# A two-block network on one core: rope and query norm worked in other places, head pairs, and steps moved

## The chip, the cores and the metric

The program runs on one core of one Trainium2 chip. The metric is the device time of one execution in microseconds (us). The engines are TensorE (PE, with its weight loads PEld), VectorE (DVE), ScalarE (ACT), GpSimd (POOL) and SyncE (SP), which here only issues DMAs. Each engine works through its own queue in the order in which the program was written; SP's DMAs are one queue too.

## The reference

The input is 256 rows of 1024 numbers. Block one is attention plus PEER, block two has two layers. What matters here:

```python
# block one, attention half
q = (rms_norm(cq, cq_norm) @ w_uq).reshape(b, s, 8, 96)
kv = (rms_norm(ckv, ckv_norm) @ w_ukv).reshape(b, s, 8, 128)
k = concat([k_nope, broadcast(k_pe)], -1)        # 64 + 32, k_pe shared by the heads
q, k = rms_norm(q, q_norm), rms_norm(k, k_norm)  # over the 96 of a head
q, k = (concat([z[..., :64], rope(z[..., 64:], positions)]) for z in (q, k))
mla = chunk_causal_softmax_attention(q, k, v)    # beside it a stick-breaking attention, 8 heads of 64
x = x + concat([rms_norm(sb), rms_norm(mla)]) @ w_o
x = x + peer_ffn(rms_norm(x), ...)
# block two, layer 0: differential attention of 6 heads of 128, and a Fourier part of 256 columns
o = rmsnorm(o, subln_g) * (1 - lambda_init)      # each head by itself
x = x + gate * (concat([o, fourier_groups(f)]) @ w_out)
x = x + gate * swiglu(modulate(rmsnorm(x)))      # 2816 wide
# layer 1: convolution mixer and the same FFN; shift, scale and gate are silu(c) @ ada_w + ada_b
```

## The kernel before, in words

Activations lie transposed: 128 features on the partitions, 8 tiles of 256 rows (`xT`). Each product of full precision is three fast ones: every weight tile of 128x1024 is loaded by SP (`_load`, a ring of four), rounded on ScalarE (`_hi`) and its remainder taken on VectorE (`_lo`); `next_w` (L650) hands out the next tile of the order in `plan` (L532) and emits the casts of the tiles that follow, `self.los` remainders ahead. An output tile is then 24 matmuls. The code is written for a manual schedule: program order is queue order on each engine.

`first_mixer` (L835). `Pre` norms `xT` (L365): the first `raws` output tiles are computed from rows that are not yet normalized, while the norm is worked out, and are multiplied by the row factor `r` afterwards; later tiles read the normalized rows `hh`, `hl`. Six tiles come first: three of the query latent `cq`, two of the key and value latent `ckv`, and the shared rope key `kpe`, the sixth. Then four tiles of the stick-breaking values (48 matmuls of 512 columns). `rope_tables` (L771) is a generator of eight steps that works out sine and cosine of the angles; a step of it is emitted at each `next(rope)`, and `pre.side` emits one inside the first tile.

The attention itself is ordered by `weave` (L253): a main stream (weights in the order of `MAINS`) and tasks (the norms of queries and keys of two heads, `qk_norm` L1077, softmax heads `mla` L1102, stick-breaking heads) that a planner places into one order by a model of the engines' times. `qk_norm` squares 112x512 on ScalarE, sums with a product over ones on TensorE, takes logarithm and exponential over 112x512 and scales on VectorE; for queries it adds rope on VectorE and GpSimd.

`diff` (L1429) is the differential mixer, with the same planner: keys and second values, Fourier, then output tiles of `ev_out` are the main stream; units of heads are tasks. A pair of heads is normed by `pair`. The last two output tiles come after the planned part, in `acc_last` (L718). `ada` (L1375) is a generator of 48 steps, each one load of 512 KB and one VectorE pass, for the modulation vectors of layer 1; its steps are called out at places in `diff` and `ffn` (L1679), each `next(steps)`. `ffn` runs 22 rounds of two up tiles and one down tile and ends with `acc_last`; the first one also makes the 81 diagonal weights of the convolution and sets up the norm (`Pre`) of the mixer after it.

## Time and profile before

| what | value |
| --- | --- |
| time, median of 3 runs | 1707.84 us (1704.6 to 1708.96) |
| the profiled execution, its own time | 1705.88 us |
| its span | 1704.1 us |
| TensorE busy | 1642.9 us, 96% |
| VectorE busy | 1335.9 us, 78% |
| ScalarE busy | 1012.8 us, 59% |
| GpSimd busy | 321.9 us, 19% |

The span is from the first instruction to the last; the run's own time has 1.8 us around it. Busy time of TensorE is modelled at the ends of matmuls, so a matmul's row can be longer than its distance to the next one. Times in rows count from the span's start. Tiles are named by the program's names; `a` is the arena that most tiles share, so neighbours tell which one it is.

### The profile page before, as it was taken

How to read it: one execution, taken by the hardware profiler on the slowest of the kernel's cores; microseconds unless marked ns; L12 is line 12 of the kernel's file. 1: busy time of each engine (PE TensorE's matmuls, PEld its weight loads, DVE VectorE, ACT ScalarE, POOL GpSimd, SP SyncE). 2: the span in 40 equal slices, each digit the busy share in tenths (PEclk: the TensorE clock that was granted, in tenths of full speed). 3: DMA queues.
4: the chain of work that ended last, by engine and by line, in shares of the span. 5: the costliest groups of instructions: out<-in, count | busy, mean ns of one | idle time of the engine just before them, and what ended most of it. 6: DMA issues, size and time to landing. Idle time of an engine off the chain costs nothing.

```text
span 1704.1 us, 33577 instructions
## 1 busy us (share of the span) xinstructions
PE 1642.9 (96%) x12984; PEld 1577.0 (93%) x12984; DVE 1335.9 (78%) x2379; ACT 1012.8 (59%) x1932; POOL 321.9 (19%) x201
## 2 busy tenths in 40 slices
PE   6999999999999999999999999998999989899998
PEld 6878999999999999999999998787999989789997
DVE  6688899987788876778788879977878799875555
ACT  5875554567777765444555564565556677564444
POOL 1021589920000000000000015311000047310000
PEclk9999999999999999999999999999999999999999
DMA  5433455554444457767887753143898733245553
GB/s 179 129 112 100 143 171 177 183 169 162 161 162 162 162 169 244 244 235 247 301 299 278 259 195 134 56 149 134 296 307 313 260 112 100 65 158 186 186 186 124
DMA packets 88111, 315.66 MB, mean 185 GB/s; under 512 B 10000, under 2 KB 11024, under 8 KB 87696
## 3 DMA queue, kind: packets, MB, share of 16 engines
q1 hardware_dynamic: 87952, 313.51, 54.6%
q8 instruction: 104, 1.70, 0.4%
q14 instruction: 55, 0.45, 0.1%
HBM read 312.03 MB, written 1.05 MB: 184 GB/s over the span
## 4 chain that ended last, share of the span: by engine, by line
PE 73%; DVE 11%; ACT 6%; DMA 4%; POOL 3%; issue 2%; SPq 0%; DVEq 0%; ACTq 0%; POOLq 0%
PE mm L178 42%; PE at L178 30%; DVE a L208 9%; ACT a L208 3%; POOL a L208 3%; DMA a<-in_peer_v_dram 2%; ACT wh L208 2%; DMA a<-in_w_dram 1%; DMA a<-in_peer_u_dram 1%; DVE adaw L208 0%; DVE xT L208 0%; ACT L208 0%; DVE gb L208 0%; PE at L183 0%; DMA a<-in_w_in_dram 0%
## 5 line engine op out<-in xcount | busy, mean ns | idle before, releaser
L178 PE MATMUL mm<-a,wh 128*128 128x256 f32 (+3 forms) x4752 | 658.7, 288 | 19.6 <-DVE a L208 7.4
L208 ACT ACTIVATE wh<-a 128x1024 fp32r<-128x1024 f32 (+3 forms) x491 | 515.1, 1053 | 267.0 <-DMA a<-in_w_dram 116.9
L208 DVE TENSOR_TENSOR a<-a,wh 128x1024 fp32r<-128x1024 f32 (+2 forms) x436 | 539.0, 1243 | 124.2 <-ACT wh L208 123.2
L178 PEld LDWEIGHTS mm<-a,wh 128*128 128x128 f32 (+1 forms) x4752 | 602.7, 189 | 35.3 <-DVE a L208 10.1
L178 PE MATMUL mm<-a,a 128*128 128x256 f32 (+5 forms) x2616 | 413.1, 296 | 10.8 <-DVE a L208 7.7
L178 PEld LDWEIGHTS mm<-a,a 128*128 128x128 f32 (+1 forms) x2616 | 357.6, 191 | 22.2 <-DVE a L208 5.7
L178 PE MATMUL at<-a,wh 128*128 128x256 f32 x2152 | 283.0, 282 | 8.8 <-DVE a L208 4.9
L178 PEld LDWEIGHTS at<-a,wh 128*128 128x128 f32 x2152 | 268.2, 189 | 11.1 <-DVE a L208 5.7
L208 POOL TENSOR_TENSOR a<-a 128x256 f32<-128x256 f32 (+4 forms) x44 | 71.6, 1628 | 852.0 <-ACT a L208 826.6
L178 PE MATMUL at<-a,a 128*128 128x256 f32 (+6 forms) x1288 | 209.1, 296 | 3.3 <-DVE sz L208 1.9
L178 PEld LDWEIGHTS at<-a,a 128*128 128x128 f32 (+2 forms) x1288 | 170.6, 189 | 17.4 <-issue 12.8
L208 ACT ACTIVATE a<-a 128x256 fp32r<-128x256 f32 (+8 forms) x225 | 103.1, 469 | 115.4 <-DVE a L208 86.0
L208 POOL TENSOR_TENSOR a<-a,a 128x256 f32<-128x256 f32 (+4 forms) x65 | 77.8, 1201 | 476.6 <-ACT a L208 422.5
L208 POOL TENSOR_TENSOR a<-a,wh 128x1024 fp32r<-128x1024 f32 x54 | 148.6, 2773 | 15.4 <-ACT wh L208 15.2
L208 DVE TENSOR_TENSOR a<-a,a 128x256 fp32r<-128x256 f32 (+6 forms) x188 | 108.3, 577 | 28.7 <-ACT a L208 23.8
L208 ACT ACTIVATE a<-mm 128x256 f32<-128x256 f32 (+30 forms) x174 | 60.6, 352 | 96.5 <-PE mm L178 96.2
L178 PE MATMUL at<-fgh,wh 128*128 128x256 f32 x352 | 87.3, 284 | 2.2 <-ACT wh L208 2.2
L178 PE MATMUL at<-fgl,wh 128*128 128x256 f32 x352 | 87.1, 284 | 0.0
L208 ACT ACTIVATE oh<-oh,rest 128x128 f16<-128x128 f16 x256 | 81.1, 399 | 0.0
L208 DVE TENSOR_TENSOR a<-a,at 128x204 f32<-128x204 f32 (+54 forms) x115 | 36.6, 355 | 48.9 <-PE at L178 42.6
L208 DVE TENSOR_TENSOR fs<-fs,mm 128x256 f32<-128x256 f32 x38 | 16.0, 421 | 74.5 <-PE mm L178 69.0
L178 PEld LDWEIGHTS at<-fgh,wh 128*128 128x128 f32 x352 | 67.1, 191 | 2.7 <-ACT wh L208 2.7
(157 smaller groups left out, 1559.4 us busy)
## 6 DMA issues: line engine op xcount, KB each, us to landing
a<-in_w_dram SPq DMA_DIRECT2D x132, 512.0 KB, 3.5
a<-in_peer_u_dram SPq DMA_DIRECT2D x128, 512.0 KB, 3.3
a<-in_peer_v_dram SPq DMA_DIRECT2D x128, 512.0 KB, 4.2
adaw<-in_ada_dram SPq DMA_DIRECT2D x48, 512.0 KB, 4.4
a<-in_ada_dram SPq DMA_DIRECT2D x48, 512.0 KB, 5.0
a<-in_pw_dram SPq DMA_DIRECT2D x24, 512.0 KB, 3.3
a<-in_w_pq_dram SPq DMA_DIRECT2D x16, 512.0 KB, 3.2
a<-in_ev_qkf_dram SPq DMA_DIRECT2D x14, 512.0 KB, 3.3
```

Source lines behind the costliest of these rows:

```text
L178: return self.engine.matmul(out, w, x, **kw)
L208: return f(*args, **kw)
```

## The change

It makes six edits. The rope key is computed as a sixth raw tile and scaled by `r` on VectorE; the angle steps move out of the first tiles into the four value tiles. The keys of two heads come from one product of 128 weight columns. The query norm's factor is no longer multiplied into the queries: it is computed per row as two columns and used as the scale of the softmax. In the differential mixer the last two heads are normed singly, the order of output tiles becomes `ORDER`, with Fourier tile 7 held back to the sixth place, and part of the last two output tiles enters the planned order. The steps of `ada` move from output tiles to the second values and Fourier tiles, end one round earlier in the first FFN, and the set-up of the norm behind that FFN moves one round forward.

```diff
+ORDER = (6, 0, 1, 2, 3, 7, 4, 5)
-            add("ev_out", D, (i + 6) % KD)
+            add("ev_out", D, ORDER[i])
-    def acc_last(self, acc, cs):
+    def last_steps(self, acc, cs):
...
             for low in range(2):
                 for k in (2 * b, 2 * b + 1):
                     self.acc_part(acc, ws[i], *cs[i], k, low, False, i == 1)
+                if b < 3 and i == 0:
+                    yield
+
+    def acc_last(self, *args):
+        for _ in self.last_steps(*args):
+            pass
 # first_mixer
-        pre = Pre(..., raws=5)
+        pre = Pre(..., raws=6)
-        pre.side, pre.rate = rope, RATEA
+        pre.rate = RATEA
-        self.los = 2
...
-        next(rope, None)
-        next(rope, None)
...
-        pk = self.tile_t(hh, hl, m=QR)
-        self.copy(kpe[64:QR], pk[64:QR])
+        pk, _ = pre.tile()
+        next(rope, None)
+        nc.vector.tensor_tensor(kpe[64:QR], pk[64:QR], r[64:QR], op=ALU.mult)
+        self.los = 2
...
+                if kk == 0:
+                    next(rope, None)
...
-                    for p in range(4):
+                    for b in range(2):
                         ps = self.bank()
                         for j in range(2):
-                            self.gemm_t(ps[:64, j * T:(j + 1) * T], w, (2 * p + j) * 64, 64, 512, range(2), ckvh, ckvl)
+                            self.gemm_t(ps[:, j * T:(j + 1) * T], w, (2 * b + j) * P, P, 512, range(2), ckvh, ckvl)
+                            if j == 0:
+                                yield
-                        nc.vector.tensor_copy(km[:64, 2 * p:2 * p + 2].rearrange("p a t -> p (a t)"), ps[:64])
+                        for o in range(2):
+                            nc.vector.tensor_copy(km[:64, 4 * b + o:4 * b + o + 3:2], ps[o * 64:(o + 1) * 64].rearrange("p (a t) -> p a t", a=2))
...
-                    self.copy(qm[:, 2 * p:2 * p + 2].rearrange("p a t -> p (a t)"), ps[:QR])
+                    nc.scalar.activation(sqs[p], ps[:QR], AF.Square)
+                    self.copy(qm[:, 2 * p:2 * p + 2].rearrange("p a t -> p (a t)"), ps[:QR], scale=self.vec("q_norm", rows=QR))
 # q_norm, in place of the query half of qk_norm (k_norm keeps the other half)
+        ps = self.bank()
+        for n in range(4):
+            self.pe.matmul(ps[:, 2 * n:2 * n + 2], sq[:, n * P:(n + 1) * P], self.con("ones", QR, 2), start=True, stop=True)
+        rq = rqs[:, 2 * p:2 * p + 2].rearrange("p h g e -> p (h g e)")
+        self.act(rq, ps[:, :8], AF.Ln, bias=epsq)
+        self.act(rq, rq, AF.Exp, scale=-0.5)
 # mla
-        nc.vector.tensor_scalar(mx[:, 2:4], mx[:, 0:2], -sc, None, op0=ALU.mult)
+        nc.vector.scalar_tensor_tensor(mx[:, 2:4], mx[:, 0:2], -1.0, rqs[:, h, :, 0], op0=ALU.mult, op1=ALU.mult)
-            self.act(e[:, reg[g]], ps[:, reg[g]], AF.Exp, scale=sc, bias=mx[:, 2 + g:3 + g], accum_out=z[:, g:g + 1])
+            self.act(e[:, reg[g]], ps[:, reg[g]], AF.Exp, scale=rqs[:, h, g, 0:1], bias=mx[:, 2 + g:3 + g], accum_out=z[:, g:g + 1])
 # diff, main stream
-            yield from values(1, "mm")
+            for n, _ in enumerate(values(1, "mm")):
+                if 1 < n < 7:
+                    next(steps, None)
+                yield
             for i in range(2):
                 self.copy(fT[:, i], self.tile_t(lh, ll))
+                next(steps, None)
                 yield
+            next(steps, None)
             yield from self.fourier(fw, fT, m, an, mh, ml)
             acc.extend(self.bank() for _ in range(4))
             for k in order[:6]:
                 if k < 6:
                     yield {("p", k // 2)}
-                next(steps, None)
                 yield from self.acc_steps(acc, self.next_w(), mh[:, k], ml[:, k], k == order[0])
+            yield {("p", 4)}
+            rest.append(self.last_steps(acc, [(mh[:, k], ml[:, k]) for k in order[6:]]))
+            for _ in range(6):
+                next(rest[0])
+                yield
...
-            self.split(f2(mh), f2(ml), o, cut=T)
+            self.split(f2(mh), f2(ml), o)
...
-            if h % 2 == 1:
-                tasks.append(Task(("p", h // 2), pair(h // 2), [("o", h - 1), ("o", h)]))
+            if h in (1, 3):
+                tasks.append(Task(("p", h // 2), normal(h - 1, 2), [("o", h - 1), ("o", h)]))
+            elif h > 3:
+                tasks.append(Task(("p", h), normal(h, 1), [("o", h)]))
...
-        self.acc_last(acc, [(mh[:, k], ml[:, k]) for k in order[6:]])
+        for _ in rest[0]:
+            pass
 # ffn
-            if layer == 0 and f >= 2:
+            if layer == 0 and 2 <= f < NF - 1:
                 next(steps, None)
+            if layer == 0 and f == NF - 1:
+                for _ in steps:
+                    pass
+                self.pre = Pre(...)
             if f == NF:
-                if layer == 0:
-                    self.pre = Pre(...)
                 self.acc_last(acc, cs[-2:])
...
-            if layer == 0 and 2 <= f < NF:
-                for q in range((f - 2) * len(diag) // (NF - 2), (f - 1) * len(diag) // (NF - 2)):
+            if layer == 0 and 2 <= f < NF - 1:
+                for q in range((f - 2) * len(diag) // (NF - 3), (f - 1) * len(diag) // (NF - 3)):
```

In the conformer, the loop that ran the rest of the steps is gone.

## Rows read from the trace of the kernel before

**Rows 1.** The page's chain that ended last, shares by engine.
```profile
PE 73%; DVE 11%; ACT 6%; DMA 4%; POOL 3%; issue 2%; SPq 0%; DVEq 0%; ACTq 0%; POOLq 0%
```

**Rows 2.** Stretches: length, busy time of engines (instructions), clock, DMA share, rate.
```profile
35.10:41.70 6.60, 5.33 (x18) 4.78 (x19) 5.43 (x17) 2.83 (x6) 0.08 (x1) 0.50 0.20 56
...
1158.10:1164.70 6.60, 5.25 (x23) 5.08 (x24) 4.23 (x7) 2.63 (x4) 0.97 (x1) 0.50 0.01 2
...
1362.90:1366.10 3.20, 3.20 (x17) 3.20 (x17) 1.92 (x5) 0.98 (x3) 0.00 (x0) 0.50 0.22 68
```

**Rows 3.** TensorE's timeline, rope key and values: start, length, instruction, idle before.
```profile
29.55 1.40 PE L178 MATMUL mm<-a,wh 128*112 128x256 f32 x9
...
36.38 0.98 PE L178 MATMUL mm<-a,wh 128*112 128x256 f32 x3 [2.47 <-DVE a L208]
...
40.21 1.42 PE L178 MATMUL at<-wh,a 128*128 128x512 f32 x2
...
50.72 0.50 PE L178 MATMUL at<-a,a 128*128 128x512 f32 x1 [0.53 <-DVE a L208]
```

**Rows 4.** VectorE's timeline there.
```profile
18.30 0.18 DVE L208 CAST a<-a 128x64 f32<-128x64 int32 x1
...
27.64 2.89 DVE L208 SCALAR_TENSOR_TENSOR a<-a,a 128x320 f32<-128x320 f32 x4
...
36.24 0.99 DVE L208 TENSOR_TENSOR a<-a 128x64 f32<-128x64 f32 x4
...
49.44 1.23 DVE L208 TENSOR_TENSOR a<-a,wh 128x1024 fp32r<-128x1024 f32 x1 [3.22 <-ACT wh L208]
```

**Rows 5.** Timeline of the attention norms, TensorE, ScalarE and VectorE.
```profile
61.94 0.63 PE L178 MATMUL mm<-a,wh 128*64 128x256 f32 x4
...
70.59 0.69 ACT L208 ACTIVATE a<-mm,eps 112x512 f32<-112x512 f32 x1
...
77.56 0.75 DVE L208 SCALAR_TENSOR_TENSOR a<-a,vecs,a 112x512 f32<-112x512 f32 x1
...
85.76 2.74 PE L178 MATMUL mm<-a,cons 112*112 112x512 f32 x6
```

**Rows 6.** TensorE's timeline around the lambda product of two columns.
```profile
1008.74 0.28 PE L178 MATMUL at<-lam,cons 128*128 128x2 f32 x2
...
1008.88 2.18 PE L178 MATMUL mm<-a,wh 128*128 128x258 f32 x16
```

**Rows 7.** TensorE's timeline, a wait in the attention.
```profile
102.41 0.89 PE L178 MATMUL at<-a,a 114*128 114x128 f32 x4 [1.89 <-DVE sz L208]
```

**Rows 8.** Stretches of attention, second values, Fourier and output tiles.
```profile
60.00:90.00 30.00, 29.57 (x190) 23.71 (x189) 16.27 (x25) 26.08 (x45) 0.00 (x0) 1.00 0.41 113
...
1080.00:1107.00 27.00, 27.00 (x140) 23.43 (x140) 24.77 (x50) 16.42 (x34) 7.67 (x6) 1.00 0.19 62
...
1117.00:1128.50 11.50, 11.47 (x60) 8.76 (x58) 4.43 (x11) 6.54 (x18) 0.84 (x1) 1.00 0.13 46
...
1128.50:1152.30 23.80, 23.58 (x175) 21.53 (x174) 23.48 (x43) 14.70 (x27) 0.92 (x1) 1.00 0.59 204
```

**Rows 9.** Timeline of the differential mixer's end.
```profile
1150.71 1.06 ACT L208 ACTIVATE wh<-a 128x1024 fp32r<-128x1024 f32 x1 [3.63 <-DMA a<-in_ev_out_dram]
...
1155.43 1.12 PE L178 MATMUL at<-a,cons 128*128 128x512 f32 x2 [1.13 <-ACT a L208]
...
1159.30 0.20 ACT L208 ACTIVATE a<-mods 128x16 fp32r<-128x16 f32 x1
...
1159.45 1.47 PE L178 MATMUL mm<-a,wh 128*128 128x256 f32 x4 [2.89 <-ACT a L208]
```

**Rows 10.** Timeline of the first FFN's end.
```profile
1361.10 0.18 DVE L208 TENSOR_TENSOR a<-mods,a 128x16 fp32r<-128x16 f32 x1 [1.64 <-ACT a L208]
...
1362.47 0.55 PE L178 MATMUL at<-fgh,a 128*128 128x256 f32 x2 [2.69 <-DVE a L208]
```

**Rows 11.** SP's queue, its waits, 1010 to 1172: us in total, times, longest.
```profile
SPq L1381 <- DVE a L208: 36.2, 7, 13.8
```

More of the change, by code (lines that the diff above doesn't have):

```diff
@@ L852, in first_mixer @@
         mh, ml = ar(0, KD, T, dt=F32R), ar(U, KD, T, dt=F32R)
-        pre = Pre(self, self.xT, lambda k: self.vec("attn_norm", k), None, 0, ar(13 * U, 3, 2, T), r, scratch, raws=5)
+        pre = Pre(self, self.xT, lambda k: self.vec("attn_norm", k), None, 0, ar(13 * U, 3, 2, T), r, scratch, raws=6)
         for j in range(4):
@@ L1002, in first_mixer @@
         tasks = []
+        part = lambda p, i: ar(2 * U + (2 * p + i) * 512 if p < 2 else 11 * U + (2 * p + i - 4) * 512, 512)[:QR]
+        sqs = [part(p, 1) for p in range(4)]
+        rqs = self.t(sp, [P, HEADS, 2, 2], tag="rqs")
+        epsq = self.t(sp, [P, 1], tag="epsq")
+        nc.vector.memset(epsq, EPS * QK)
         for p in range(4):
-            for i, (n, which, x) in enumerate((("k", "k_nope", km), ("q", "q_norm", qm))):
-                s = ar(2 * U + (2 * p + i) * 512 if p < 2 else 11 * U + (2 * p + i - 4) * 512, 512)[:QR]
-                tasks.append(Task((n + "_norm", p), self.qk_norm(s, which, x, p, qe, None if i else kpe), [(n, p)], "qk"))
+            tasks.append(Task(("k_norm", p), self.k_norm(part(p, 0), km, p, kpe), [("k", p)], "qk"))
+            tasks.append(Task(("q_norm", p), self.q_norm(sqs[p], qm, p, qe, rqs, epsq), [("q", p)], "qk"))
         for h in range(HEADS):
-            tasks.append(Task(("m", h), self.mla(sp, qe[:QR + 2], ke[:QR + 2], vm, mlo, h), [("q_norm", h // 2), ("k_norm", h // 2), "vm"], "mla"))
+            tasks.append(Task(("m", h), self.mla(sp, qe[:QR + 2], ke[:QR + 2], vm, mlo, h, rqs), [("q_norm", h // 2), ("k_norm", h // 2), "vm"], "mla"))
             if h % 4 == 3:
@@ L1075, in stick, with k_norm @@
         self.freed(i)
-    def qk_norm(self, sq, which, x, p, ext, kpe=None):
+    def k_norm(self, sq, x, p, kpe):
         nc = self.nc
-        flat = lambda v: v[:, 2 * p:2 * p + 2].rearrange("p a t -> p (a t)")
         v3 = lambda ap: ap.rearrange("p (a t) -> p a t", a=2)
-        xs = flat(x)
-        n = QR if kpe is None else 64
-        nc.scalar.activation(sq[:n], xs[:n], AF.Square)
-        if kpe is not None:
-            nc.scalar.activation(v3(sq[64:]), self.bc(kpe[64:QR], 2), AF.Square)
+        xs = x[:, 2 * p:2 * p + 2].rearrange("p a t -> p (a t)")
+        nc.scalar.activation(sq[:64], xs[:64], AF.Square)
+        nc.scalar.activation(v3(sq[64:]), self.bc(kpe[64:QR], 2), AF.Square)
         yield
@@ L1091, in qk_norm, with q_norm @@
         yield
-        nc.vector.scalar_tensor_tensor(xs, xs, self.vec(which, rows=QR), sq, op0=ALU.mult, op1=ALU.mult)
-        if kpe is not None:
-            return
+        nc.vector.scalar_tensor_tensor(xs, xs, self.vec("k_nope", rows=QR), sq, op0=ALU.mult, op1=ALU.mult)
+    def q_norm(self, sq, x, p, ext, rqs, epsq):
+        nc = self.nc
+        v3 = lambda ap: ap.rearrange("p (a t) -> p a t", a=2)
+        xs = x[:, 2 * p:2 * p + 2].rearrange("p a t -> p (a t)")
+        ps = self.bank()
[5 more added lines that the diff above has]
+        yield
         for o, i in ((slice(64, 96), slice(96, P)), (slice(96, QR), slice(64, 80))):
@@ L1535, in diff @@
             pass
-        order = (6, 7, 0, 1, 2, 3, 4, 5)
+        order = ORDER
         acc = []
@@ L1563, in pair @@
             ps, i = self.at()
+            ps = ps[:, :n * T]
             self.pe.matmul(ps, self.con("ones"), s, start=True, stop=True)
@@ L1571, in pair @@
             yield
-            f2 = lambda x: x[:, 2 * b:2 * b + 2].rearrange("p a t -> p (a t)")
-            self.split(f2(mh), f2(ml), o, cut=T)
+            f2 = lambda x: x[:, b:b + n].rearrange("p a t -> p (a t)")
+            self.split(f2(mh), f2(ml), o)
+        rest = []
         aT, parts = {}, {}
@@ L1743, in conformer @@
         sp = self.pool("Gs", 1, ctx=ctx)
-        hh, hl, diag, steps = self.hh, self.hl, self.diag, self.steps
+        hh, hl, diag = self.hh, self.hl, self.diag
         y = ar(23552, KD, T)
@@ L1917, in conformer @@
             if k == KD // 2:
-                for _ in steps:
-                    pass
                 self.table(AF.Exp)
```

15 lines of the change are left out of this document (8 added, 7 removed).

## The prediction

> **What bounds the kernel now.** I read the page's chain first, then TensorE's own timeline, then the other engines at those places. The chain that ended last is TensorE for 73% of the span [rows 1], and its timeline shows it working nearly throughout: the time is TensorE's stream, and an edit pays only where it shortens that stream or closes a hole in it. The holes are few. A view of stretches by clock shows what a hole costs beyond itself: behind three holes at places that this change touches the granted clock stands at 0.50 (the 1.2 GHz level), twice for 6.6 us and once for 3.2 us [rows 2]. So there are three places to work out, and one where matmuls themselves go: the shared rope key near 30 us [rows 3, 4], the attention norms near 60 to 90 us [rows 5], the end of the differential mixer near 1150 us [rows 8, 9], and the end of the first FFN near 1360 us [rows 10].
>
> **Part 1, raw rope key and angles beside values (20 to 60 us).** Now the key's tile reads normalized rows: it starts at 29.55 and waits for VectorE, 2.47 us in the last of its waits, and the value matmuls start only at 40.21 [rows 3]. VectorE is late because three pieces of angle work stand between its normalization steps: ten small operations (18.30 to 19.82, 1.5 us), a range reduction (26.92 to 30.44, 3.5 us, its long part is the row) and a second one (36.24 to 38.87, 2.6 us) [rows 4]. After the change the tile reads raw rows. TensorE: 29.55 plus 24 matmuls at 0.119 (2.9) plus the four passes of the second norm (0.9) is 33.3, 6.9 us before 40.21. That is the upper end, for the 7.6 us of angle work are only moved. They now stand in VectorE's queue among the remainders of the value weights. Between the key tile (32.4) and the fourth value weight's remainder VectorE has: the key's scaling 0.3, query-latent scaling 0.9, three weight remainders at 1.23 [rows 4] 3.7, the two reductions 6.1, other latent scaling 1.7, and a wait of about 1.6 for ScalarE's cast: 14.3, so 46.7. Before, the same remainder let TensorE go on at 50.72 [rows 3]. The gain there is 4.0 us, not 6.9; a replay of the four queues in order with these durations gives 5.4. TensorE then stands idle some 3 to 5 us before the fourth value tile, and a fall of the clock like those of [rows 2] would take up to 1.6 back. I take 4.0, bounds 1 and 6.9. The other cover lost is ScalarE's: its two table loads and eight sines now stand between weight casts, which the replay includes. The key's scaling on VectorE replaces a ScalarE copy; its own next wait, the broadcast DMA of the rope key, comes later and nobody is near it.
>
> **Part 2, attention norms (53 to 145 us).** Keys two heads at once: 24 matmuls of width 64 go, 0.119 each by their spacing (four in 0.63 with the last one's tail [rows 5]), 2.8 us. The copies are still four. Query norm: four matmuls of 512 columns over the ones matrix go, three of them (six passes) take 2.74 us [rows 5], so 3.65 for four; sixteen with two columns come. The nearest row is the lambda product with two columns: from its start to the next matmul's start is 0.14 us [rows 6], so 2.2. Together TensorE loses 4.2 us. ScalarE's logarithm and exponential over 112x512 become 128x8: 0.69 [rows 5] against 0.20 for the nearest narrow one, 128x16 [rows 9], so eight times 0.46, some 3.5 us less; VectorE's scaling, 0.75 [rows 5], goes four times, 3.0 us. The square reads PSUM before the copy instead of SBUF after it: one bank is held some 0.6 us longer, at no cost while four are there. In softmax a constant scale becomes a column: same instructions, same count.
> A rule of the Trainium skill speaks against this part: the page "TensorE: Matmul & The Clock Gate", section "LDWEIGHTS (loading the stationary operand)", has a weight load take columns/1.2 ns whatever the moving width. By it (an estimate) sixteen two-pass products with 128 weight columns are 32 x 107 ns = 3.4 us, the query side saves 0.2 and not 1.4, and the sum below would be 1.2 us smaller. The trace does not agree: two passes stand 0.14 us apart [rows 6], not 0.21, so the sum goes by the row.
> How much reaches the end? Until about 100 us TensorE is full, so its 4.2 count; afterwards it waits for VectorE, first 1.89 us at 102.41 [rows 7], and the lead must be carried by VectorE, which has 3.0 us less to do. I take 3.0. Bounds: 0 (VectorE keeps its pace) and 7.4 (the 4.2, the hole of 1.89, and half of a 3.2 us stretch at half clock behind it). The planner also sets a new order, so a new hole like that one is possible: minus 3.4 is the end below nothing.
>
> **Part 3, end of the differential mixer.** Now after the last output product TensorE waits 1.13 for the copy and square of two heads and 2.89 for logarithm, exponential, scaling and split [rows 9], 4.0 together. Then it runs from 1159.45 to 1164.70 at half clock [rows 2], losing half of 5.25, 2.6. Sum 6.6, the upper bound. Afterwards the last norm is over 256 columns, not 512: copy to first matmul takes 3.0 instead of 4.7 by scaling each step with the width. And 18 of the 24 matmuls of head 4's output tile (2.1 us) can be issued behind the last output product, because only head 5 is then missing; the Fourier tile 7 only trades its place with heads 0 to 3. The hole shrinks to about 4.0 - 1.7 - 2.1 = 0.2, with slack for the hops between engines to 1; should the clock fall behind it all the same, the 2.6 stay lost. What can spoil it further: the new step takes the casts and loads of the next FFN's weights into the queue before the last head's chain. ScalarE already stood 3.63 us for a weight's DMA there, with the head's copy right behind [rows 9]. Lower bound 0. I take 5.0.
> The steps of the modulation vectors (one load of 512 KB on SP, one VectorE pass of 1.22 and 0.08) move: six go from the output tiles (1128.5 to 1152.3, VectorE busy 23.48 of 23.8) and eight come to the second values and the Fourier tiles (VectorE 24.77 of 27.0, then 4.43 of 11.5 in the Fourier) [rows 8]. That is 10.4 us into a stretch with about 9 free, and 7.8 out of the tail. TensorE has no hole in 1080 to 1152 now, so I cost the move at nothing; its cover is the planner's filler (value and output tiles) and the idle 7 us in the Fourier. If that cover fails, units of heads 3 and 4 run up to 1.4 us later.
>
> **Part 4, end of the first FFN.** Now VectorE runs a modulation step (1.22) late, then a small split that waits 1.64 for ScalarE (behind a table load), and only then the last weight remainder; TensorE waits 2.69 [rows 10] and then runs 3.2 us at half clock [rows 2], 1.6 lost: 4.3. With the steps ended one round earlier and the new norm's set-up in front of the last split, VectorE's queue after 1357.2 is multiply 0.34, set-up 0.5, split (after ScalarE's cast) to 1358.5, remainder 1.2: 1359.7, against a need at 1359.6. The hole nearly goes. Take 4.0, bounds 2 and 4.3. The 81 diagonal copies are spread over 19 rounds instead of 20, a fifth of a copy more per round on a ScalarE that is half idle, and the drained loop in the conformer has nothing left to drain: both nothing.
>
> **Sum.** 4.0 + 3.0 + 5.0 + 4.0 = 16.0. The profiled execution took 1705.88 (span 1704.1), so the changed one would take 1689.9; that execution lay 1.96 below the median of the runs shown, 1707.84, and against the median the forecast is 1691.8.
>
> **Rivals.**
> First, the front's lead is lost in attention: VectorE and ScalarE are the pace from 30 to 50 us and again from 100 to 140, so angles beside values only swap one wait for another. For it: VectorE's waits for ScalarE casts beside values, 3.22 [rows 4]. Against it: VectorE is busy 16.27 of 30 us from 60 to 90 [rows 8], so what comes earlier can be taken earlier. Parts 3 and 4 remain: 1707.84 - 9 = 1698.8.
> Second, the tail of the mixer keeps its hole since the next weights' casts go first: part 3 gives 0 to 1, total 11.5, 1696.3. For it the 3.63 us row, against it that the weights' buffers are then free for longer.
> Third, the other side: SP's queue. Each moved modulation load waits on SP until VectorE has left its buffer, 36.2 us in 7 waits around the mixer [rows 11], and weight loads stand behind it. Were the eight loads among values and Fourier tiles to cost TensorE 3.63 each (ScalarE's wait [rows 9]), 29 us would be lost: 1707.84 - 16 + 29 = 1721. It decides from 2.0 us a load. Against it: six such loads stand among output tiles now and TensorE shows no hole there; weights are loaded several tiles ahead.
> That the change does not do what it says would show as holes unchanged at 36, 1155 and 1362 us; no reason speaks for it in the last, which is plain order.
>
> **Chances.** Forecast 0.56 (own range 1687 to 1695), first rival 0.18, second 0.16, third 0.05, and 0.05 for more than forecast, with the hole at 102 us also gone (1684). The range from 1683 to 1701 takes in the first two rivals and most of what they would be together. A measurement here tells 0.3% (5.1 us) from no change. Faster by more: all but the third and some of the two first rivals together, 0.92; within: 0.04; slower: 0.04.
>
> **What would show it.** Right: no wait of the rope key's tile, values starting at about 33 us, one wait before the fourth value tile; query norm products spaced by 0.14 us; full clock through 1160 and 1363 us; the last head's norm over 256 columns. Wrong: a new hole with half clock behind it between 1080 and 1150, or ScalarE standing for an FFN weight's DMA before the last head's copy; a hole of 5 us beside values whose half clock reaches into the first query tile.

## The result, and the profile after

| | before | after |
|---|---|---|
| median of the runs (9 each) | 1706.68 us | 1697.04 us |
| range of the runs | 1703.16 to 1708.96 | 1693.52 to 1700.32 |
| ratio, 95% interval | | 0.9948 [0.9938, 0.9958] |
| the profiled execution, its span | 1705.88, 1704.1 | 1694.07, 1692.3 |

The change is faster by 0.52%, 9.6 us by the medians; the profiled pair differs by 11.8. The forecast was 16.0 less, 1691.8 us, with a range of 1683 to 1701 that holds the time. I cut both traces at TensorE's own landmarks, the start of the first matmul of each stage, and set the four parts beside their stages. Every other stage agrees within 0.8 us.

| stage | before | after | gain | forecast |
|---|---|---|---|---|
| start to the first query tile (part 1) | 53.1 | 48.9 | 4.2 | 4.0 |
| first query tile to PEER's first matmul on one-hot rows (`at<-oh`) (part 2) | 317.2 | 310.8 | 6.4 | 3.0 |
| second values to the first FFN matmul (part 3) | 86.9 | 91.1 | -4.2 | 5.0 |
| first FFN, first output matmul to the last (part 4) | 182.9 | 177.8 | 5.1 | 4.0 |

The page's engine line and chain after, which answer to [rows 1]:
```profile
PE 1636.0 (97%) x12986; PEld 1574.0 (93%) x12986; DVE 1333.6 (79%) x2379; ACT 1009.4 (60%) x1935; POOL 325.5 (19%) x198
PE 71%; DVE 14%; ACT 6%; DMA 4%; POOL 2%; issue 2%; SPq 0%; DVEq 0%; ACTq 0%; POOLq 0%
```
TensorE is still the stream that sets the time; VectorE's share of the chain has risen from 11% to 14%, so more of that chain runs through VectorE.

Stretches of the kernel after, columns as in [rows 2, 8] (length, busy time of PE, PEld, DVE, ACT, POOL, granted clock, DMA share, rate):
```profile
42.90:49.50 6.60, 5.00 (x13) 4.05 (x14) 3.89 (x8) 6.02 (x13) 0.00 (x0) 0.50 0.02 4
...
1069.00:1096.00 27.00, 26.64 (x136) 24.13 (x135) 26.42 (x49) 14.37 (x31) 8.66 (x6) 0.94 0.37 130
1096.00:1106.50 10.50, 10.50 (x69) 8.96 (x69) 10.30 (x17) 6.12 (x12) 3.39 (x2) 1.00 0.77 273
...
1120.00:1145.00 25.00, 23.51 (x159) 20.26 (x158) 16.57 (x30) 14.78 (x31) 0.00 (x0) 1.00 0.28 89
...
1155.60:1158.80 3.20, 3.04 (x13) 2.87 (x14) 1.67 (x6) 0.80 (x4) 0.00 (x0) 0.50 0.00 0
1070.30:1073.50 3.20, 3.20 (x11) 3.20 (x11) 3.17 (x5) 1.37 (x3) 2.70 (x2) 0.50 0.00 0
```
Read it against [rows 8]. In the second values VectorE was busy 24.77 of 27 and is now 26.42 of 27, and 10.30 of the next 10.5: the modulation steps went into this stretch and the room that it had is gone. In the output tiles it now idles (16.57 of 25). The clock stands at 0.50 in three places named here: behind the values' wait, behind the tail's waits, and at 1070.3, where TensorE is busy throughout.

TensorE's timeline of the kernel after, values, query norm and attention, which answers to [rows 3, 5, 6, 7]:
```profile
29.78 1.02 PE L179 MATMUL mm<-a,cons 128*128 128x256 f32 x4
30.45 0.82 PE L179 MATMUL at<-wh,a 128*128 128x512 f32 x2
...
41.92 0.73 PE L179 MATMUL at<-wh,a 128*128 128x512 f32 x2 [2.71 <-ACT wh L209]
44.50 0.80 PE L179 MATMUL at<-a,a 128*128 128x512 f32 x1 [1.85 <-DVE a L209]
...
72.33 0.95 PE L179 MATMUL mm<-cons,a 112*128 112x2 f32 x8
73.14 1.66 PE L179 MATMUL mm<-a,wh 128*128 128x256 f32 x12
...
102.59 0.55 PE L184 MATMUL at<-cons,me 128*128 128x128 f32 x3
```
VectorE's row for the fourth value tile's remainder:
```profile
43.22 1.22 DVE L209 TENSOR_TENSOR a<-a,wh 128x1024 fp32r<-128x1024 f32 x1
```
The rope key waits for nothing and the values start at 30.45 instead of 40.21; all of the waiting is now in front of and inside the fourth value tile, where TensorE goes on at 44.50, when this remainder is done. Eight two-column passes (four products) take 0.81 us from start to start. The hole of 1.89 us at 102 is not there; a smaller one of 1.27 stands at 113.07.

TensorE's holes in the mixer of the kernel after, against [rows 9]:
```profile
1108.31 1.16 PE L179 MATMUL mm<-a,a 128*128 128x128 f32 x8 [1.47 <-ACT a L209]
...
1133.32 1.99 PE L179 MATMUL at<-daT,a 128*128 128x256 f32 x8 [1.49 <-ACT daT L209]
...
1147.17 1.89 PE L179 MATMUL at<-daT,a 128*128 128x256 f32 x8
...
1153.08 0.70 PE L179 MATMUL at<-a,cons 128*128 128x256 f32 x2 [2.60 <-ACT a L209]
...
1155.76 1.47 PE L179 MATMUL mm<-a,wh 128*128 128x256 f32 x4 [1.74 <-ACT a L209]
```
ScalarE there:
```profile
1146.96 1.06 ACT L209 ACTIVATE wh<-a 128x1024 fp32r<-128x1024 f32 x1 [0.89 <-DMA a<-in_w_dram]
1151.26 1.06 ACT L209 ACTIVATE wh<-a 128x1024 fp32r<-128x1024 f32 x1 [3.23 <-DMA a<-in_w_dram]
1152.22 0.37 ACT L209 ACTIVATE a<-at 128x256 f32<-128x256 f32 x1
```
The last head's product starts at 1147.17 and its eight matmuls take 1.89. Its copy is the third row of ScalarE, at 1152.22: in front of it stands a cast of the next FFN's weight, which waits 3.23 us for its DMA. That load was issued late:
```profile
1146.89 0.33 SPq L600 DMA_DIRECT2D a<-in_w_dram  x1
```
SP had stood 2.8 us in front of it until TensorE had left the buffer.

VectorE and then TensorE at the end of the first FFN, after, against [rows 10]:
```profile
1350.31 0.17 DVE L209 TENSOR_TENSOR a<-mods,a 128x16 fp32r<-128x16 f32 x1
...
1352.96 1.23 DVE L209 TENSOR_TENSOR a<-a,wh 128x1024 fp32r<-128x1024 f32 x1 [0.81 <-ACT wh L209]
```
```profile
1355.16 0.40 PE L179 MATMUL at<-fgh,a 128*128 128x256 f32 x2
1355.40 0.57 PE L179 MATMUL mm<-a,wh 128*128 128x258 f32 x2
```
The small split no longer waits, the last weight remainder is there, and TensorE goes from the last output matmul to the conformer without a wait and at full clock.

### The profile page after: what moved, and what is told of

It is laid out like the page before. It is cut to its first block, busy times and chain, and to the rows that moved or that the text cites. A ratio compares the mean times of both kernels' runs of the same rounds, so it can differ in the third digit from the quotient of the medians.

```text
span 1692.3 us, 33577 instructions
## 1 busy us (share of the span) xinstructions
PE 1636.0 (97%) x12986; PEld 1574.0 (93%) x12986; DVE 1333.6 (79%) x2379; ACT 1009.4 (60%) x1935; POOL 325.5 (19%) x198
## 4 chain that ended last, share of the span: by engine, by line
PE 71%; DVE 14%; ACT 6%; DMA 4%; POOL 2%; issue 2%; SPq 0%; DVEq 0%; ACTq 0%; POOLq 0%
PE mm L179 41%; PE at L179 30%; DVE a L209 10%; ACT a L209 3%; POOL a L209 2%; DMA a<-in_peer_v_dram 2%; ACT wh L209 2%; DMA a<-in_w_dram 1%; DMA a<-in_peer_u_dram 1%; DVE praw L209 1%; DVE dmx L209 1%; DVE xT L209 1%; DVE adaw L209 0%; DVE gb L209 0%; DVE de L209 0%
## 5 line engine op out<-in xcount | busy, mean ns | idle before, releaser
L209 DVE TENSOR_TENSOR a<-a,wh 128x1024 fp32r<-128x1024 f32 (+2 forms) x436 | 533.3, 1230 | 121.3 <-ACT wh L209 115.9
L179 PEld LDWEIGHTS at<-a,a 128*128 128x128 f32 (+2 forms) x1288 | 171.5, 190 | 16.6 <-issue 10.5
L209 ACT ACTIVATE a<-a 128x256 fp32r<-128x256 f32 (+7 forms) x220 | 99.1, 460 | 109.2 <-DVE a L209 87.1
L209 POOL TENSOR_TENSOR a<-a,a 128x256 f32<-128x256 f32 (+5 forms) x62 | 80.3, 1300 | 427.6 <-ACT a L209 336.4
L209 DVE TENSOR_TENSOR a<-a,a 128x256 fp32r<-128x256 f32 (+7 forms) x189 | 111.7, 592 | 22.3 <-ACT a L209 17.5
L209 ACT ACTIVATE a<-mm 128x256 f32<-128x256 f32 (+29 forms) x173 | 60.2, 352 | 95.8 <-PE mm L179 95.7
```

Of the source, the lines that this page charges most:

```text
L179: return self.engine.matmul(out, w, x, **kw)
L209: return f(*args, **kw)
```

## The experiments

Ratios are to the kernel before, in runs on the same chip; the changed kernel stands at 0.9948 [0.9938, 0.9958] by the same measure. "Second values to FFN" is the stage of the table above.

**The next weights' casts behind the last head (late_casts).** In the step that takes the last output tiles:
```
-        ws = [self.next_w(i == 0, i) for i in range(2)]
-        (load and cast the weights that follow)
+        ws = [self.next_w(i == 0 and not late, i) for i in range(2)]
         for n, (b, i) in enumerate(...):
+            if n == (3 if late else 0): (load and cast the weights that follow)
```


> The changed kernel, but the casts of the first two weight tiles of the FFN are emitted behind the planned part, as in the kernel before, and not with the first step of the last two output tiles. Theory A (the cast waiting 3.23 us for an FFN weight's DMA, which stands in ScalarE's queue ahead of head 5's copy, makes the hole in the tail): the copy follows the last output product within 0.4 us, the two holes of 2.60 and 1.74 shrink to under 2 together, span 1692.3 - 3 = about 1689, ratio to before about 0.993. Rival B (the norm chain itself makes the hole): two holes of about 4 together remain, span within 1 us of 1692.3.


Measured: 1693.82 us, 0.9930 [0.9915, 0.9944]; second values to FFN 88.6 instead of 91.1. TensorE's tail:
```profile
1153.64 0.59 PE L179 MATMUL at<-a,cons 128*128 128x256 f32 x2
...
1156.21 0.96 PE L179 MATMUL mm<-a,wh 128*128 128x256 f32 x3 [1.75 <-ACT a L209]
```
The wait of 2.60 for the head's copy is gone, the norm's own chain of 1.75 stays, and the clock does not fall behind it. So the casts did hold up the last head, as theory A had it, though the span of 1692.0 is rival B's. Upstream, in the second values, the wait of 0.36 at 1091 has become one of 1.92 with half clock behind it; query_old, whose mixer is the changed kernel's, has 1.94 there, so it is not the casts' doing:
```profile
1093.19 0.44 PE L179 MATMUL mm<-a,a 128*128 128x384 f32 x1 [1.92 <-DVE a L209]
```
The intervals of this kernel and the changed one overlap a little; alone it is worth some 3 us. How far this stage varies by itself: the six executions that share the changed kernel's mixer (the changed one, key_normed, query_old, keys_singly, front_undone and ffn_end_back) took 89.2 to 92.0, so 88.6 is just outside. The waits of about 1.48 (twice) and 1.74 stand in all six; the one in front of the last head's statistics goes from 1.58 to 2.60.

**The old tail (tail_undone).** Heads 4 and 5 normed as a pair, both Fourier tiles early, the last output tiles whole:
```
-ORDER = (6, 0, 1, 2, 3, 7, 4, 5)
+ORDER = (6, 7, 0, 1, 2, 3, 4, 5)
...
-            if h in (1, 3): normal(h - 1, 2) ... elif h > 3: normal(h, 1)
+            if h % 2 == 1: normal(h - 1, 2)
...
-        for _ in rest[0]: pass
+        self.acc_last(acc, [(mh[:, k], ml[:, k]) for k in order[6:]])
```


> The changed kernel with the old tail: heads 4 and 5 normed as a pair, Fourier tile 7 second again, last two output tiles behind the planned part; steps stay moved. Theory A (single heads gain nothing as written, for the early casts eat it): tail hole 4.0 and 2.6 of half clock as before against 4.3 and 1.5 now, span about 1693. Rival C (single heads and held tile did pay, and the steps' move lost the time elsewhere): span 1697 or more.


Measured: 1696.79 us, 0.9947 [0.9932, 0.9961], the time of the changed kernel; second values to FFN 91.9. Its profiled execution is the longest of its five runs (span 1699.5), and the stage from PEER to the lambda product, which has no edit, took 4.7 longer in it than in the changed kernel, so the span decides nothing between theory A and rival C. Its tail has the holes of [rows 9] again:
```profile
1156.94 1.13 PE L179 MATMUL at<-a,cons 128*128 128x512 f32 x2 [1.13 <-ACT a L209]
...
1160.95 1.11 PE L179 MATMUL mm<-a,wh 128*128 128x256 f32 x4 [2.89 <-ACT a L209]
```
Single heads and the held Fourier tile, as written, neither gained nor lost: 1.13 and 2.89 became 2.60 and 1.74.

**The modulation steps back among the output tiles (steps_back).**
```
-            for n, _ in enumerate(values(1, "mm")):
-                if 1 < n < 7: next(steps, None)
-                yield
+            yield from values(1, "mm")
...
             for k in order[:6]:
+                next(steps, None)
```
The two steps left over go into rounds 2 and 3 of the FFN.


> The changed kernel with the modulation steps back among the six output tiles of the planned part (none beside second values and Fourier tiles; the two steps fewer run in rounds 2 and 3 of the first FFN). Theory D (the steps moved beside second values delay units there): the holes of 1.47 and 1.49 us near 1108 and 1133 and the stretch at half clock near 1070 go, span 1688 to 1689. Rival E (the planner's new order makes those holes, not the steps): holes of the same size remain, span 1692 or more, since VectorE is full again in the tail.


Measured: 1693.32 us, 0.9918 [0.9903, 0.9933]; second values to FFN 84.2. TensorE runs through the places where the changed kernel waits 1.47 and 1.49:
```profile
1110.03 4.86 PE L179 MATMUL mm<-a,a 128*128 128x128 f32 x32
...
1141.08 1.89 PE L179 MATMUL at<-daT,a 128*128 128x256 f32 x8
```
These are the Fourier's products and the last head but one. The steps' place among the second values and the Fourier copies cost time; its ratio lies below that of the changed kernel without overlap. The span of 1695.2 is not the 1688 to 1689 of theory D, but the two holes that it named are gone. The tail's own hole was 2.29 us here and the clock did not fall behind it. The first FFN's stage took 183.2 instead of 177.8: the two steps left over and a half-clock stretch at 1196 stand in it (180.8 in late_steps, which has the same two steps).

**Part 1 undone (key_normed).** Normalized rope key, its angle steps beside the norms again:
```
-        pre = Pre(..., raws=6)
+        pre = Pre(..., raws=5)
...
-        pre.rate = RATEA
+        pre.side, pre.rate = rope, RATEA
... (the angle steps and self.los = 2 back in their old places)
-        pk, _ = pre.tile()
-        next(rope, None)
-        nc.vector.tensor_tensor(kpe[64:QR], pk[64:QR], r[64:QR], op=ALU.mult)
+        pk = self.tile_t(hh, hl, m=QR)
+        self.copy(kpe[64:QR], pk[64:QR])
```


> The changed kernel with part 1 undone: rope key from normalized rows as a sixth tile behind five raw ones, angle steps among the first tiles. Theory F (part 1 gives what is left of the 10.4 us lead at the end of the first mixer after 4.2 us of matmuls): span 1692.3 + 6 = about 1698. Rival G (part 1 gives the 4.0 of the prediction, the rest comes from a hole near 102 us that went): span about 1696, and the hole near 102 stays away without part 1.


Measured: 1704.33 us, 0.9992 [0.9982, 1.0002]: 0.44% or 7.5 us slower than the changed kernel. The first query tile starts 4.0 later, and the attention behind it takes 3.4 more (314.2 against 310.8); a hole like that of [rows 7] is back, which rival G excluded, and the loss is more than theory F had:
```profile
99.61 0.68 PE L179 MATMUL at<-a,a 114*128 114x128 f32 x3 [1.33 <-DVE sz L209]
```

**Query norm as before (query_old).** The norm over a ones matrix, the scaling of the queries on VectorE, a constant scale in the softmax:
```
-        for n in range(4):
-            self.pe.matmul(ps[:, 2 * n:2 * n + 2], sq[:, n * P:(n + 1) * P], self.con("ones", QR, 2), ...)
+        self.pe.matmul(ps[:QR], self.con("ones", QR, QR), sq, start=True, stop=True)
...
+        nc.vector.scalar_tensor_tensor(xs, xs, self.vec("q_norm", rows=QR), sq, op0=ALU.mult, op1=ALU.mult)
```


> The changed kernel with the query norm as before: square from SBUF, one product of 512 columns over ones, logarithm and exponential over 112x512, scaling on VectorE, constant scale in the softmax. Theory H (TensorE is the pace until 100 us): 1.4 us of matmuls come back, stretch from first query tile to last stick matmul 94.1 + 1.4 = 95.5, ratio to before about 0.996. Rival I (VectorE's 3.0 and ScalarE's 3.5 us are the pace): +3 or more, 0.997. Rival J (nothing of it reaches the end): +0.5 at most.


Measured: 1701.99 us, 0.9980 [0.9968, 0.9991], 5.5 us slower than the changed kernel (theory H had 1.4, rival I 3 or more); the attention stage has 316.8. The hole near 102 is back, and the clock falls to 0.50 at 106.7 behind it:
```profile
105.28 0.61 PE L184 MATMUL at<-cons,me 128*128 128x128 f32 x3 [2.23 <-DVE me L209]
```

**Keys one head at a time (keys_singly).**
```
-            for b in range(2): (two heads' keys in one tile of 128 rows, two copies)
+            for p in range(4):
+                for j in range(2):
+                    self.gemm_t(ps[:64, j * T:(j + 1) * T], w, (2 * p + j) * 64, 64, 512, range(2), ckvh, ckvl)
+                nc.vector.tensor_copy(km[:64, 2 * p:2 * p + 2]..., ps[:64])
```


> The changed kernel with the keys one head at a time, 24 matmuls of width 64 more. Theory H: 2.8 us come back in the stretch from first query tile to last stick matmul, 94.1 + 2.8 = 96.9, ratio to before about 0.9965. Rival J (the stretch is paced by chains of the heads, not by TensorE): under +1, ratio within 0.001 of the changed kernel's.


Measured: 1701.77 us, 0.9976 [0.9966, 0.9986], 4.8 us slower than the changed kernel, more than the 2.8 of its matmuls; the attention stage has 318.6, in an execution with a long stretch at half clock. Again:
```profile
99.21 1.55 PE L179 MATMUL at<-a,a 114*128 114x128 f32 x8 [1.56 <-DVE sz L209]
```

**Parts 1 and 2 undone together (front_undone).** The three edits above in one kernel.


> Parts 1 and 2 undone together (normalized rope key with its angle work in the old places, query norm over the ones matrix, keys one head at a time); mixer tail and FFN end as in the changed kernel. Theory N (the three share one gain, because an undone one only hands its loss to the planner's next hole): together they cost what the two traces differ there, start to PEER 10.7 us, so 1697.0 + 10.7 = about 1707.7, and the stretch from the first query tile to PEER has 317 us as in the kernel before. Rival (their costs add: 7.5 + 5.4 + 4.8 = 17.7 us by the single runs): about 1714.7, that stretch 324 us, slower than the kernel before.


Measured: 1707.84 us, 1.0009 [1.0000, 1.0018], 0.61% or 10.4 us slower than the changed kernel (10.8 by the medians), as the theory of one shared gain had it (1707.7); the rival's 1714.7 is far outside. The attention stage has 317.2, that of the kernel before. Its trace shows the old waits in their old places:
```profile
36.54 0.98 PE L179 MATMUL mm<-a,wh 128*112 128x256 f32 x3 [2.48 <-DVE a L209]
...
102.58 1.27 PE L179 MATMUL at<-a,a 114*128 114x128 f32 x4 [1.89 <-DVE sz L209]
```
Two things follow. The single losses, 7.5, 5.5 and 4.8, are not three gains: they add to 17.8, and all three edits undone cost 10.4. What is counted more than once is in part the hole near 102 us: undone singly, each edit brings one back there (1.33, 2.23 and 1.56), and all together bring one of 1.89, which explains 3.2 of the 7.4. The rest is not shown. Half clock follows such a hole at once only in query_old; in keys_singly it comes at 127 and 165 us, and in key_normed nowhere in the attention. And since this kernel keeps parts 3 and 4, those two together are worth nothing, or a little less: what the FFN's end gives, the mixer's end takes.

**The FFN's end as before (ffn_end_back).**
```
-            if layer == 0 and 2 <= f < NF - 1:
+            if layer == 0 and f >= 2:
                 next(steps, None)
-            if layer == 0 and f == NF - 1: (rest of the steps; self.pre = Pre(...))
             if f == NF:
+                if layer == 0: self.pre = Pre(...)
```


> The changed kernel with the first FFN as before: set-up of the next norm in its last round, diagonal copies over 20 rounds, steps asked for until the end (though all but one are already done). Theory K (set-up behind a table load is what holds the last weight remainder): the hole of 2.7 us with half clock behind it returns, stretch of that FFN 177.8 + 4.3 = 182.1, ratio to before 0.997. Rival L (the late modulation step of 1.22 us was the cause, and it ends earlier here too): the hole is 1.4 or less, no half clock, stretch under 180.


Measured: 1698.77 us, 0.9954 [0.9938, 0.9971], an interval that overlaps the changed kernel's. The trace is plainer: the FFN takes 182.6 instead of 177.8, with the wait of [rows 10] again and half clock from 1357.4:
```profile
1357.91 0.58 PE L179 MATMUL at<-fgh,a 128*128 128x256 f32 x1 [2.76 <-DVE a L209]
```
By this pair of profiled executions part 4 is worth 4.8; by the runs 1.7, with no clear sign. All the traces bear it out: the ten executions with the new end and no extra steps took 177.1 to 178.9, the two with the old end 182.6 and 182.9.

**Steps beside the Fourier, casts behind (late_fourier).** The casts as in the first experiment; five steps between the Fourier's units and three with the first three output tiles:
```
-            yield from self.fourier(fw, fT, m, an, mh, ml)
+            for _ in self.fourier(fw, fT, m, an, mh, ml):
+                next(steps, None)
+                yield
...
+                if k in (0, 1, 6): next(steps, None)
```


> The changed kernel with late casts of the FFN's weights and with the eight modulation steps placed where VectorE was idle: five beside the Fourier product, three with the first three output tiles (none beside second values, none beside Fourier's input tiles). Theory A and D together: no hole over 1 us between 1070 and 1140, tail holes under 2.5 together; stretch from second values to the FFN 82 to 85 (91.1 in the changed kernel, 88.6 with late casts alone, 84.2 with steps back alone), ratio to before 0.989 to 0.991. Rival E (planner's order makes the holes): stretch 87 or more.


Measured: 1689.06 us (1687.19 to 1692.62), 0.9908 [0.9889, 0.9927], faster than the kernel before and the changed one; second values to FFN 83.0. Its tail as a stretch (columns as above), and TensorE's and ScalarE's rows:
```profile
1145.00:1160.00 15.00, 14.31 (x106) 12.96 (x105) 12.01 (x25) 10.83 (x20) 2.80 (x2) 1.00 0.50 169
```
```profile
1126.00 0.66 PE L184 MATMUL at<-cons,de 128*128 128x128 f32 x4 [1.73 <-ACT a L209]
...
1146.85 0.59 PE L179 MATMUL at<-a,cons 128*128 128x256 f32 x2
```
```profile
1147.48 0.47 ACT L209 ACTIVATE a<-at,eps 128x256 f32<-128x256 f32 x1 [2.75 <-PE at L179]
1149.39 2.00 ACT L209 ACTIVATE wh<-a 128x1024 fp32r<-128x1024 f32 x2
```
Here the tail is what the change describes: TensorE goes on with head 4's tile while the last head's norm runs, both casts come behind the chain, and the clock stays at 1.00. What is left is a wait of 1.73 among the first output tiles. ScalarE's row just before it:
```profile
1124.22 1.06 ACT L209 ACTIVATE wh<-a 128x1024 fp32r<-128x1024 f32 x1 [5.09 <-DMA a<-in_ev_out_dram]
```
This is the third rival on a small scale. The load of that weight left SP only at 1119.73, right behind a modulation load that had waited 3.8 us for VectorE; steps_fourier and fourier_tail show the same, with waits of 1.81 and 1.88.

**The steps alone (steps_fourier).** The same places for the steps, the casts where the change has them.


> The weight casts of the next FFN stay where the change has them; only the modulation steps move: five into the Fourier tiles, three to the first three output tiles, none to the second values. Theory (two separate losses in the mixer's end, the casts at its tail and the steps in the second values): the holes near 1108 and 1133 us are gone or under 1 us, the tail holes of about 2.6 and 1.7 us stay; second values to FFN 86 to 88 us, the time about 1693. Rival (late casts are what made the best version, the steps hardly matter): the same as the changed kernel, 1697, with 91 us there.


Measured: 1695.45 us, 0.9939 [0.9925, 0.9953]; second values to FFN 91.2. The stage is the rival's, and the time lies between the two: no gain that can be told from the changed kernel. The holes near 1108 and 1133 are gone or under 1 us, as the theory had it, but its tail is worse. ScalarE and then TensorE there:
```profile
1149.48 1.06 ACT L209 ACTIVATE wh<-a 128x1024 fp32r<-128x1024 f32 x1 [3.12 <-DMA a<-in_w_dram]
1152.18 1.06 ACT L209 ACTIVATE wh<-a 128x1024 fp32r<-128x1024 f32 x1 [1.64 <-DMA a<-in_w_dram]
```
```profile
1155.06 1.47 PE L179 MATMUL mm<-a,wh 128*128 128x256 f32 x4 [3.85 <-ACT a L209]
```
TensorE came earlier to the tail and waited longer there: both casts now wait for their loads in front of the last norm, which gives 3.85 in one piece, and half clock from 1154.3 to 1161.1.

**Late casts with the steps among the output tiles (late_steps).** The edits of late_casts and steps_back together.


> Weight casts of the next FFN behind the planned part, and the steps back among the six output tiles with two more in the FFN's early rounds. Theory (the two losses are separate and add up): 83 to 84 us from second values to FFN with no tail hole above 1 us; FFN 178 us or some us more by its two extra steps; 1689 to 1692. Rival (with the steps among output tiles VectorE is late for the last heads, so the late casts gain nothing there): 84 to 86 us and the time of the version with the steps back alone, 1693.


Measured: 1691.60 us, 0.9910 [0.9895, 0.9924]; second values to FFN 83.3, as the theory had it, but with a tail hole of 2.28 us at 1147.71, which it hadn't; the clock did not fall behind it. It can't be told from late_fourier, nor from steps_back alone.

**The new places of the steps with the old tail (fourier_tail).** The edits of tail_undone, and the steps as in late_fourier.


> The old tail of the mixer (heads 4 and 5 normed as a pair, both Fourier tiles early, the last output tiles whole behind the planned work) with the modulation steps in the Fourier tiles and the first three output tiles. Theory (single heads and the held tile are worth their price only once the next weights' casts stand behind the last head): 4 to 5 us slower than the same steps with single heads and late casts (1689.1), so 1693 to 1694, about 87 us from second values to FFN, with the old pair of holes of about 1 and 3 us at the tail and half clock behind them. Rival (where the steps stand was the whole loss, the tail hardly matters): 1689 to 1691, 83 to 84 us there.


Measured: 1694.89 us, 0.9937 [0.9923, 0.9951], 5.8 above late_fourier by the medians, a little more than the 4 to 5 of the theory, with intervals that just touch; second values to FFN 91.0, four more than it said. The holes of the old tail and half clock from 1150:
```profile
1125.32 0.66 PE L184 MATMUL at<-cons,de 128*128 128x128 f32 x4 [1.88 <-ACT a L209]
...
1148.58 1.12 PE L179 MATMUL at<-a,cons 128*128 128x512 f32 x2 [1.14 <-ACT a L209]
1152.59 1.47 PE L179 MATMUL mm<-a,wh 128*128 128x256 f32 x4 [2.88 <-ACT a L209]
```

Set side by side, second values to FFN in the mixer's versions (us):

| | steps in the second values and Fourier input tiles | beside the Fourier and the first output tiles | among the output tiles |
|---|---|---|---|
| old tail | 91.9 | 91.0 | 86.9 (the kernel before) |
| single heads, casts first | 91.1 (the change) | 91.2 | 84.2 |
| single heads, casts late | 88.6 | 83.0 | 83.3 |

With casts late the stage is 83 us wherever the steps are, as long as they are not among the second values. With the casts first only steps_back is that short. There the planner's order has both casts behind the last head's copy and square, and neither waits for a DMA:
```profile
1149.48 0.72 ACT L209 ACTIVATE a<-a 128x256 fp32r<-128x256 f32 x2 [0.55 <-DVE a L209]
1150.11 2.00 ACT L209 ACTIVATE wh<-a 128x1024 fp32r<-128x1024 f32 x2
```
The second instruction of the first row is the square. Only the logarithm and what follows it stand behind the casts there, and TensorE waited 0.84 for them. Why the planner's order came out so was not traced.

## Why the prediction was right, and where it was wrong

**What bounds the kernel** held: TensorE's stream with its holes and the half clock behind them. The four places were the right ones, and all of the gain and loss lies in them.

**Part 1 was right** in its mechanism, and in size in part by luck: forecast 4.0, measured 4.2 at the first query tile, and 4.0 when undone alone. The lead at the start of the values is 9.8, where 6.9 was worked out (values at 33.3, measured 30.45), and shrinks in front of the fourth value tile, as worked out. There VectorE's remainder let TensorE go on at 44.50 instead of the 46.7 of the sum: 6.2 us ahead of the kernel before, not 4.0. The half clock behind that wait took 2.0 of it back by the first query tile, 6.60 us at 0.50 with TensorE busy for 5.00 (2.5 lost in all), where I had counted up to 1.6. The two misses nearly cancel. The half clock lasts 0.6 us into the first query tile, which I had named as a sign of being wrong, with waits of 2.71 and 1.85 ahead of it. Nine executions with this front reach the first query tile at 48.9 to 50.4, so the pair's 4.2 is the upper end of 2.8 to 4.2; they reach PEER at 359.6 to 360.7, against 370.4 before.

**Part 2 was undersized**, 3.0 against 6.4, inside its bounds (up to 7.4), and one step of it was wrong. The two-column products stand 0.20 us apart (eight passes in 0.81), not 0.14: sixteen take 3.2, and the query side saves TensorE 0.4, not 1.4. I had taken the distance from one lone product to the wide matmul behind it [rows 6] for that of a row of them. The rule of the Trainium skill that I set aside there (page "TensorE: Matmul & The Clock Gate", section "LDWEIGHTS (loading the stationary operand)": a weight load takes columns/1.2 ns whatever the moving width) gives 0.21 by an estimate, and this trace agrees with it.
The gain came from the other side. Add up, for each matmul of that stage, the time to the next start less the median of its kind: this excess fell from 20.5 to 17.8. Between 100 and 110 us it fell by more than that (4.15 to 0.69), and elsewhere it rose by 0.7. What went there is the hole of [rows 7], and the stretch at half clock behind it, which the prediction's list of stretches [rows 2] had left out:
```profile
103.30:106.70 3.40, 3.40 (x18) 3.31 (x16) 3.35 (x5) 2.94 (x10) 0.85 (x1) 0.50 0.00 0
```
The other 3.7 of the 6.4 is matmul work, most of it the 2.8 and 0.4 of the two edits. So what I gave 0.05 as "the hole at 102 us also gone" is what happened. That it needs all three edits (the earlier start, the query's smaller chain, the shorter keys) is what the experiments on the front show, since each one undone brings a hole back there; I had summed parts 1 and 2 as if each had a price of its own. The first rival (the front's lead lost in attention) is wrong: with part 1 undone (key_normed) the attention takes 3.4 longer, on top of the 4.0 at the start.

**Part 3 is the step that failed.** "The hole shrinks to about 4.0 - 1.7 - 2.1 = 0.2, with slack for the hops between engines to 1", then "I take 5.0", and "I cost the move at nothing": measured -4.2, below the lower bound of 0. The traces give the sum. At the tail the holes of 1.13 and 2.89 and the 2.6 of half clock, 6.6, became 2.60, 1.74 and 1.5 (half of 3.04): 5.8, so 0.8 gained. Upstream came waits of 0.36 (at 1091), 1.47 and 1.49, 3.3, and 1.6 for half clock at 1070. 0.8 - 3.3 - 1.6 is -4.1. Other executions of the same mixer lose 2.3 to 5.1 against the one trace of the kernel before, so the sign holds and the size is rough. Two causes:
- The casts of the next FFN's weights stand in front of the last head's chain. This is the second rival, down to the row that it was read from; I gave it 0.16 because "the weights' buffers are then free for longer". They weren't: the second load was issued at 1146.89, when TensorE had left its buffer, the cast's turn came at 1148.0, and it waited 3.23. late_casts shows it, and steps_fourier shows it growing. The norm itself became shorter about as forecast: from the copy to the first matmul behind it 3.5 us, 5.1 before (forecast 3.0 and 4.7).
- The modulation steps do not fit between the second values. I had worked out 10.4 us into about 9 free, and then called it covered by filler and the idle 7 in the Fourier. VectorE went to 26.42 of 27, and ScalarE's copies for the Fourier and for the last head but one, which had been in time, came late by 1.5 each, about the 1.4 that I had named "if that cover fails". That the steps' place brings these two waits is shown: both stand in all seven executions with the steps there and single heads, and neither in steps_back or late_steps. With the casts late, taking the steps out is worth 5.3 (88.6 to 83.3). That a full VectorE is the way from one to the other is argued only: the waits end on ScalarE, and the planner's order differs there too.

The half clock at 1070 has no wait ahead, and other executions have such a stretch elsewhere or not at all, so the last 1.6 belongs to no edit that I could name.

**The third rival**, SP's queue, did not come in the changed kernel (a mild form of it is in late_fourier, above): by SP's waits from 1000 to 1160 (us in total, times, longest) it waited less for VectorE in front of the modulation loads than the 36.2 of [rows 11]:
```profile
SPq L1405 <- DVE a L209: 21.8, 6, 7.8
...
SPq L1405 <- DVE dz L209: 6.9, 2, 4.9
```

**Part 4 was right** in the mechanism and near in size in the traces: forecast 4.0, 5.1 in this pair, 4.8 with the edit undone. The runs agree in direction only, and not clearly (1.7).

**The sum** of 16.0 was 4.2 too large by the profiles and 6.4 by the medians: 3.4 too little in part 2 and 9.2 too much in part 3 make 5.8 too much, of which 1.3 comes back in parts 1 and 4, and 0.3 lies in stages without an edit. That the time is in the range is luck in part: it rests on these errors partly cancelling, and on the parts that were right.

## What to carry to other kernels

Before casts or loads for the next stage are put ahead of a last dependent chain, look at whether their data has landed by then: an engine that waits for a DMA holds back whatever stands behind it in its queue. Work that is moved should be added to the busy time of the stretch that takes it; a stretch at 24.8 of 27 has no room for eight steps of 1.3 us, though the engine that matters shows no hole there. Edits that all bring the same late engine forward can share one gain: here each of three, undone by itself, seemed to be worth 4.8 to 7.5 of the 10.4 that they are worth together, so measure them against a kernel that has none of them.

## What the runs showed of the hardware that was not expected

- The granted clock can stand at 0.50 with no wait just ahead. In the kernel after, TensorE is busy without a break and at clock 1.00 from 1045.0 to 1070.2, and then runs 3.2 us at 0.50 (the row at 1070.30 above):
```profile
1045.00:1070.20 25.20, 25.20 (x100) 17.68 (x100) 24.42 (x47) 15.88 (x35) 10.70 (x10) 1.00 0.16 47
```
  Other executions with the same code in that stretch show it at 1062.9 (tail_undone), at 1046.2 and 1059.9 (steps_back), or not at all (late_fourier).
- The same hole does not always bring the fall. In late_fourier a wait of 1.73 at 1126.00 leaves the clock at 1.00; in fourier_tail one of 1.88 at 1125.32, at the same matmul, is followed by 3.20 us at 0.50, as is one of 1.81 in steps_fourier. So the price of a hole of this size is itself, or itself and 1.6.
- Two-column products over 128 weight columns cost TensorE 0.10 us a pass, nearly the 0.119 of a pass with 256 columns [rows 5].
- Stages without an edit vary between executions: that from PEER's first matmul on one-hot rows to the lambda product took 637.6 to 642.3. An effect of 2 us in one stage of one profile is no proof by itself.
